# One expert's pair beside the small pair alone, in a mixture-of-experts stage on one core

## The chip, the cores and the metric

The kernel runs on one core of one Trainium2 chip. A core has a matrix engine (TensorE, PE in the profile), a vector engine (VectorE, DVE), an activation engine (ScalarE, ACT), GpSimd (POOL) and a queue engine (SyncE, SP) that issues the transfers here. Each runs its own instructions in order and waits for the others by semaphores. 16 DMA engines move data from HBM to the on-chip memory. The metric is the device time of one execution in microseconds (us); lower is better.

## The reference

Two layers of a backbone over 256 latent tokens with 256 context tokens, width 1024, all in float32. Each layer has a token mixer and a feed-forward part. The second layer's feed-forward part is a mixture of 8 experts, each token going to its best two:

```python
logits = (x @ router)
top_v, top_i = lax.top_k(logits, 2)
gates = einsum(softmax(top_v), one_hot(top_i, 8))
out = 0
for e in range(8):                      # wg, wu: 1024 x 3584, wd: 3584 x 1024
    out = out + gates[..., e:e + 1] * ((silu(x @ wg[e]) * (x @ wu[e])) @ wd[e])
```

It is followed by a residual and a layer norm. Only this mixture is touched by the change.

## The kernel before

**Pairs.** The tokens of each expert are gathered into blocks of up to 128, and the blocks stand in order of size, two to a pair, `a` to `d`. With the inputs measured, the first expert has more than 128 tokens and fills both blocks of pair `a` (kind 'one': up to 208 columns, one expert's weights for both blocks). Pair `b` ('whole') has two experts of up to 128 tokens, `c` ('mixed') one of up to 128 and one of up to 64, and `d` ('tiny') two of up to 32. Seven experts' weights are read, 588 transfers of 512 KB.

**Weights.** An expert's weights come in 84 units of 512 KB: 7 chunks of 512 hidden columns with 8 units each (4 of the gate matrix, 4 of the up matrix), numbered 0 to 55, and 28 units of the down matrix, 4 for each chunk. The generator `expert_halves` (L1400 on) loads them in the order of a plan into five raw buffers `rp` of 1 MB. For `b`, `c` and `d` a buffer holds the same unit of both experts (L1436); for `a` it holds the next two units of its one expert (L1428). For `a`, `b` and `c` each 512 KB is then split for precision: ScalarE rounds it to `hi` (L1413), VectorE subtracts to get `lo` (L1414). There are five buffers of each (`weight_pools(5, 5, 0)`). `d` is multiplied unsplit in float32, straight from the raw buffer, which therefore stays taken until TensorE has used it.

**Matmuls of one unit.** `b`: 12 of 512 columns (three products, hi x hi, hi x lo, lo x hi, for two blocks; L261 to L263). `c`: 10, since its small block needs two (L1514, L1515). `a`: 24 of 208 columns in the gate and up matrices (L1461), 12 of 512 in the down matrix. `d`: 8 of 256 columns on 32 columns of the array (L1590), 4 of 512 in the down matrix (L1625); the trace has two records for each. After a chunk's gate and up parts come the activation, the product, and a turning or a split (`c`: L1508, L1509, L1538, L1546, L1569, L588, L589; `a`: L1466, L1469, L255, L256; `d`: L1596, L1598, L1604).

**The order.** It is a string, `SCHEDULE[0]` for this distribution of tokens. `bu0123456` is the gate and up part of `b`, chunks 0 to 6, `bd...` its down part, `cp` starts the preparation (gathering and modulating its tokens) of `c`. Parts joined by `+` are worked on together: `merged` puts their units into one list, and by that list the weights are loaded and the matmuls written. Inside the block a scheduler then orders each engine's instructions by a model of their times, so that neighbouring units are interleaved further. When the last down part of a pair is written, its result is weighed and scattered to the tokens; for parts of a pair's down matrix the sums are kept (`partial`).

Of the kernel before, what the change touches and what calls it, by code (L numbers as in the profile page):

```python
# [28 lines left out]

ONE = 208  # L30
SCHEDULE = (
    'bu0123456 cp ap bd0123456 cu01+au0 cu23+au1 cu4 cu56+ad01 dp cd0123456+au2 du0123+au34 du456+ad234 '
    'dd0123+au56 dd45+ad56 dd6',
    'au0 bp au1 bu012 ad01 bu345 au2 bu6 cp bd0123456 au3 cu01 ad23 cu234 au4 cu56 dp cd0123456 au5 du0 '
    'ad45 du123 au6 du45 ad6 du6 dd0123456',
    'au0123456 bp ad0123456 bu0123456 cp bd0123456 cu0123456 dp cd0123456 du0123456 dd0123456',
# [89 lines left out]
def ahead(gen, n):  # L126

    q = deque()
    for item in gen:
        q.append(item)  # L130
        if len(q) > n:
            yield q.popleft()
    yield from q
# [25 lines left out]
class Net:  # L159
# [1531 lines left out]
    def partial(self, P, py):  # L1691

        nc = self.nc
        if P.kind == 'tiny':
            return
        first = P.sums is None
        if first:
            P.sums = [self.t4([128, 1024]) for _ in range(2)]
        for i in range(2):
            for hh in range(2):  # L1700
                s = P.sums[i][:, hh * 512:(hh + 1) * 512]
                if first:
                    nc.scalar.activation(s, py[i][hh], AF.Copy)
                else:
                    nc.vector.tensor_add(s, s, py[i][hh])
# [78 lines left out]
    def experts(self, routed, schedule, one=None, small=False):  # L1784

        nc, gms = self.nc, self.gms
        kinds = {0: 'whole' if one is None else 'one'}
        if small:
            kinds.update({STATIC_PAIRS - 2: 'mixed', STATIC_PAIRS - 1: 'tiny'})
        work = {'whole': self.gate_up, 'one': partial(self.gate_up_one, n=ONE if small else 256), 'mixed': self.gate_up_mixed, 'tiny': self.gate_up_tiny}

        def prep(j):
            kind = kinds.get(j, 'whole')
            return self.g_pair_prep(gms[:, j], None if j else self.long, 'whole' if kind == 'one' else kind)
        order = [[('abcd'.index(w[0]), w[1], [int(x) for x in w[2:]]) for w in t.split('+')]  # L1800
                 for t in schedule.split()]
        j0 = order[0][0][0]
        if j0:
            nc.vector.tensor_scalar_add(gms[:, j0], gms[:, 0], -256.0 * j0)
        preps = {j0: Side(prep(j0))}
        self.need(preps[j0])
        self.choices(*routed, j0)

        def m5():
            self.gate_row(1, 1, 'L', self.m5)  # L1810
            yield
        self.slow.append(Side(m5()))
        self.rate = 1.0
        span = {'u': (0, 8), 'g': (0, 4), 'h': (4, 8)}

        def units(j, w, cs):

            return [56 + 4 * c + k for c in cs for k in range(4)] if w == 'd' else \
                [8 * c + k for c in cs for k in range(*span[w])]

        def merged(parts):

            us = [units(*p) for p in parts]
            return [(i, u) for _, i, u in sorted(((k + 0.5) / len(v), i, u) for i, v in enumerate(us)
                                                 for k, u in enumerate(v))]

        def up(P, w, cs):
            for c in cs:
                if c not in P.work:
                    P.work[c] = work[P.kind](P, c)  # L1830
                    next(P.work[c])
                for _ in range(*span[w]):
                    yield
                    next(P.work[c], None)
            if w in 'uh' and cs[-1] == 6:
                P.act = P.shared = None

        steps = [t for t in order if t[0][1] != 'p']
        self.stream = ahead(self.expert_halves([(t[i][0], u) for t in steps for i, u in merged(t)], one,
                                               [j for j in kinds if kinds[j] == 'tiny']), 2)  # L1840
        pairs, sc, alpha = {}, None, ALPHA
        for n, parts in enumerate(order):
            if parts[0][1] == 'p':
                preps[parts[0][0]] = self.spawn(prep(parts[0][0]))
                continue
            last = n == len(order) - 1
            rows = [self.row(self.I[r][1]) for r in ('ln2_g', 'ln2_b')] if last else None
            gens = []
            self.tight = len(parts) > 1 and any(p[1] == 'd' for p in parts)
            for j, w, cs in parts:  # L1850
                if j not in pairs:
                    pairs[j] = self.start_pair(preps.pop(j), gms[:, j], kinds.get(j, 'whole'))
                tiny = pairs[j].kind == 'tiny'
                g = up(pairs[j], w, cs) if w != 'd' else \
                    self.down_tiny(pairs[j], cs) if tiny else self.down(pairs[j], cs, last)
                next(g)
                gens.append(g)
            for i, _ in merged(parts):
                j, w, cs = parts[i]
                try:  # L1860
                    next(gens[i])
                    continue
                except StopIteration as e:
                    py = e.value
                if w != 'd':
                    continue
                P = pairs[j]
                P.done += len(cs)
                if P.done < 7:
                    self.partial(P, py)  # L1870
                    continue
                ys, GT = self.weighed(P, py)
                sc = self.spawn(self.g_final(ys, GT, alpha, *rows) if last else self.g_scatter(ys, GT, alpha))
                alpha = 1.0
                del pairs[j], P
        self.need(sc)
        for w in list(self.side) + list(self.slow):
            self.need(w)
        self.side.clear()
        self.slow.clear()  # L1880
# [208 lines left out]
```

## Time and profile before

| | |
|---|---|
| three runs, median (lowest to highest) | 1970.03 us (1968.45 to 1970.07) |
| the profiled execution | 1970.38 us, span 1968.5 us |
| busy share of the span: PE, DVE, ACT, POOL | 96%, 69%, 54%, 3% |
| read from HBM | 515.64 MB, 262 GB/s over the span |

The profile's times count from the first instruction. The mixture begins at about 1084 us. A busy PE is counted with modelled ends, so neighbouring matmuls overlap in the rows: the cost of one is the time from its start to the start of the next. DMA share is the mean busy share of the 16 DMA engines.

### The profile page before, as it was taken

Reading aid. Unit: us, or ns where it says so; the run is one execution under the profiler, and the core shown is the slowest. Engines: PE = TensorE matmul, PEld = TensorE weight load, DVE = VectorE, ACT = ScalarE, POOL = GpSimd, SP = SyncE. Lnnn points to the kernel's source line nnn. Section 1 sums busy time; section 2 is a strip of 40 time slices with the busy share of each in tenths; the row PEclk is TensorE's granted clock in tenths of the full one; section 3 lists DMA queues with packets and bytes.
Section 4 is the critical chain, followed back from the end, with each engine's and each line's share of the span. In section 5 each row is a group of like instructions: output and inputs, shape, how many; then the busy total and the mean of one; then the engine's idle time right before and its main releaser. Section 6 shows DMA issues by size and latency. Waiting matters only on the chain. (4 is left out here: it accounts for less than half of the span.)

```text
span 1968.5 us, 28818 instructions
## 1 busy us (share of the span) xinstructions
PE 1886.0 (96%) x10399; PEld 1491.8 (76%) x10399; DVE 1348.6 (69%) x1970; ACT 1063.9 (54%) x1450; POOL 60.1 (3%) x68
## 2 busy tenths in 40 slices
PE   6999999999999999999997999999999999898995
PEld 3788877788888888878886788888887886655662
DVE  3887776688654564798777888999989885222325
ACT  3657645665322222466773877887787873211221
POOL 0100000000000000011000000000000000000000
PEclk9999999999999999999998899999999999999998
DMA  8653556576734442454440999989999999999984
GB/s 332 254 198 136 192 214 252 212 270 261 295 130 163 180 172 98 171 177 150 166 167 9 380 369 367 340 326 353 345 356 353 335 376 348 409 408 409 372 325 170
DMA packets 119022, 518.77 MB, mean 264 GB/s; under 512 B 14640, under 2 KB 15536, under 8 KB 95824
## 3 DMA queue, kind: packets, MB, share of 16 engines
q1 hardware_dynamic: 118864, 516.78, 70.3%
q8 instruction: 85, 1.39, 0.3%
q14 instruction: 73, 0.60, 0.1%
HBM read 515.64 MB, written 1.09 MB: 262 GB/s over the span
## 5 line engine op out<-in xcount | busy, mean ns | idle before, releaser
L262 PE MATMUL mm<-lo,t 128*128 128x512 f32 (+1 forms) x1560 | 608.7, 390 | 3.2 <-DVE lo L1414 1.7
L1414 DVE TENSOR_TENSOR lo<-rp,hi 128x1024 fp32r<-128x1024 f32 x420 | 492.7, 1219 | 167.9 <-ACT hi L1413 162.6
L263 PE MATMUL mm<-hi,t 128*128 128x512 f32 (+1 forms) x1560 | 603.3, 387 | 0.0
L261 PE MATMUL mm<-hi,t 128*128 128x512 f32 (+1 forms) x1560 | 584.1, 393 | 13.2 <-ACT hi L1413 6.6
L1413 ACT ACTIVATE hi<-rp 128x1024 fp32r<-128x1024 f32 (+1 forms) x420 | 424.9, 1056 | 80.7 <-PE mm L263 29.6
L255 ACT ACTIVATE hi<-raw 128x1024 fp32r<-128x1024 f32 x268 | 282.7, 1058 | 341.6 <-PE mm L263 184.5
L256 DVE TENSOR_TENSOR lo<-raw,hi 128x1024 fp32r<-128x1024 f32 x268 | 325.5, 1218 | 188.8 <-ACT hi L255 187.9
L261 PEld LDWEIGHTS mm<-hi,t 128*128 128x128 f32 x1560 | 292.0, 188 | 93.3 <-issue 17.6
L262 PEld LDWEIGHTS mm<-lo,t 128*128 128x128 f32 x1560 | 294.0, 189 | 73.7 <-DVE lo L1414 12.4
L263 PEld LDWEIGHTS mm<-hi,t 128*128 128x128 f32 x1560 | 293.9, 188 | 58.3 <-issue 1.2
L1017 PE MATMUL mm<-t,hi 128*128 128x512 f32 (+1 forms) x896 | 229.3, 345 | 0.0
L1017 PEld LDWEIGHTS mm<-t,hi 128*128 128x128 f32 x896 | 155.8, 189 | 29.1 <-issue 8.4
L1461 PE MATMUL mm<-t,hi 128*128 128x208 f32 x896 | 159.6, 280 | 5.8 <-ACT hi L1413 5.7
L1461 PEld LDWEIGHTS mm<-t,hi 128*128 128x128 f32 x896 | 136.2, 192 | 36.0 <-issue 20.6
L1017 PE MATMUL mm<-t,lo 128*128 128x512 f32 (+1 forms) x448 | 153.9, 344 | 0.0
L1461 PE MATMUL mm<-t,lo 128*128 128x208 f32 x448 | 118.2, 280 | 5.6 <-DVE lo L1414 5.6
L1461 PEld LDWEIGHTS mm<-t,lo 128*128 128x128 f32 x448 | 82.8, 193 | 14.3 <-DVE lo L1414 7.8
L1017 PEld LDWEIGHTS mm<-t,lo 128*128 128x128 f32 x448 | 84.8, 189 | 10.0
L313 POOL TENSOR_TENSOR sm<-sm,mhalf 128x1 f32<-128x1 f32 (+3 forms) x46 | 54.4, 1182 | 897.2 <-DVE sm L311 884.7
L266 PE MATMUL tr<-ident,t 128*128 128x128 f32 x376 | 59.4, 281 | 17.7 <-ACT t L344 16.1
L266 PEld LDWEIGHTS tr<-ident,t 128*128 128x128 f32 x376 | 45.7, 144 | 34.9 <-ACT t L344 19.7
L1590 PE MATMUL mm<-rp,t 128*32 128x256 f32 x896 | 70.4, 384 | 1.3 <-DMA rp<-in_expu 1.1
(287 smaller groups left out, 1686.4 us busy)
## 6 DMA issues: line engine op xcount, KB each, us to landing
rp<-in_expu SPq DMA_DIRECT2D x588, 512.0 KB
raw<-in_w_inu SPq DMA_DIRECT2D x64, 1024.0 KB
raw<-in_w_modu SPq DMA_DIRECT2D x44, 1024.0 KB
raw<-in_ffnu SPq DMA_DIRECT2D x42, 1024.0 KB
raw<-in_w_branchu SPq DMA_DIRECT2D x18, 1024.0 KB
raw<-in_w_outu SPq DMA_DIRECT2D x12, 1024.0 KB
t<-in_w_modu SPq DMA_DIRECT2D x8, 512.0 KB
t<-gd SPq DMA_DIRECT2D x7, 512.0 KB
```

Source lines behind the costliest of these rows:

```text
L255: self.nc.scalar.activation(hi, src, AF.Copy)
L256: self.nc.vector.tensor_sub(lo, src, hi.bitcast(F32))
L261: mm(out, ah, wh, start=first, stop=False)
L262: mm(out, ah, wl, start=False, stop=False)
L263: mm(out, al, wh, start=False, stop=last)
L266: self.nc.tensor.transpose(out, src, self.ident)
L313: self.nc.gpsimd.tensor_tensor(r, ve, self.mhalf[:, :n], op=OP.pow)
L1017: nc.tensor.matmul(out(t), a, x[p], start=kt + m + t % per == 0, stop=kt + m + t % per == (9 if per == 1 else 10))
L1413: nc.scalar.activation(hf, rs, AF.Copy)
L1414: nc.vector.tensor_sub(lf, rs if rv is None else rv, hf.bitcast(F32))
L1461: nc.tensor.matmul(out, a, x[p], start=kt + q + t % 2 == 0, stop=kt + q + t % 2 == 10)
L1590: nc.tensor.matmul(z[o:o + 32, :], x, raws[i][:, m, h * 256:(h + 1) * 256], start=k + m == 0, stop=k + m == 7)
```

## The change

```diff
 SCHEDULE = (
-    'bu0123456 cp ap bd0123456 cu01+au0 cu23+au1 cu4 cu56+ad01 dp cd0123456+au2 du0123+au34 du456+ad234 '
-    'dd0123+au56 dd45+ad56 dd6',
+    'bu0123456 cp bd0123456 cu0123456 dp ap cd0123456 du01+au01 du2+ad01 du34+au23 du5+ad23 du6+au4 dd0123+au56 '
+    'dd45+ad456 dd6',
...
-            return [(i, u) for _, i, u in sorted(((k + 0.5) / len(v), i, u) for i, v in enumerate(us)
+            return [(i, u) for _, i, u in sorted(((k // 2 * 2 + 1) / len(v), i, u) for i, v in enumerate(us)
                                                  for k, u in enumerate(v))]
```

Pair `a`, which stood beside `c` with three chunks up and two down and beside `d` with the rest, now stands beside `d` with all of it; `c` is worked on alone. `a` is prepared after `c`'s up part and not before `b`'s down part. The sort key of `merged` is the same now for two neighbouring units of a part, so two units of one pair are followed by two of the other. Nothing that is computed or loaded changes, only its order.

VectorE in `c`'s up part, one chunk: L1414 is a split, L1509, L1546 and L1569 belong to `c`'s activation, L1469 and L256 to `a`'s. Before:

```order
L1414 TENSOR_TENSOR lo<-rp,hi 128x1024
L1469 TENSOR_TENSOR u_12704<-u_12704,mm 128x2x208
L1469 TENSOR_TENSOR u_12706<-u_12706,mm 128x2x208
L1414 TENSOR_TENSOR lo<-rp,hi 128x1024
L1569 TENSOR_TENSOR u_12897<-u_12897,mm 128x512
L256 TENSOR_TENSOR t_13031<-u_12704,t_13030 128x2x208
L256 TENSOR_TENSOR t_13031<-u_12706,t_13030 128x2x208
L1414 TENSOR_TENSOR lo<-rp,hi 128x1024
L1509 TENSOR_TENSOR u_13083<-t_13084,mm 64x512
```

The same place now:

```order
L1414 TENSOR_TENSOR lo<-rp,hi 128x1024
L1569 TENSOR_TENSOR u_12810<-u_12810,mm 128x512
L1414 TENSOR_TENSOR lo<-rp,hi 128x1024
L1414 ISA
L1414 TENSOR_TENSOR lo<-rp,hi 128x1024
L1509 TENSOR_TENSOR u_12927<-t_12928,mm 64x512
L1414 TENSOR_TENSOR lo<-rp,hi 128x1024
L1546 TENSOR_TENSOR u_12827<-u_12827,u_12927 64x512
```

`a`'s instructions are gone from among `c`'s, and what is left is `c`'s own splits and activation (ISA sets a register).

ScalarE in `d`'s gate and up part: L1413 is a split of `a`'s weights, L1466 and L255 `a`'s activation and split, L1596 and L1604 `d`'s activation and the copy of its turned result; L1596, L1466 and L1604 wait for TensorE. Before:

```order
L1596 ACTIVATE u_15844<-mm 128x256
L1413 ACTIVATE hi<-rp 128x1024 x2
L255 ACTIVATE t_15941<-u_15718 128x2x208
L255 ACTIVATE t_15941<-u_15720 128x2x208
L1604 ACTIVATE t_15447<-tr 128x256
L1413 ACTIVATE hi<-rp 128x1024 x2
L1596 ACTIVATE u_16071<-mm 128x256
L1413 ACTIVATE hi<-rp 128x1024 x2
```

Now:

```order
L1413 ACTIVATE hi<-rp 128x1024 x3
L1596 ACTIVATE u_15066<-mm 128x256
L1413 ACTIVATE hi<-rp 128x1024
L1466 ACTIVATE u_15124<-mm 128x2x208
L1466 ACTIVATE u_15126<-mm 128x2x208
L1413 ACTIVATE hi<-rp 128x1024 x4
L1604 ACTIVATE t_14503<-tr 128x256
L255 ACTIVATE t_15299<-u_15124 128x2x208
L255 ACTIVATE t_15299<-u_15126 128x2x208
```

Where two splits stood between any two of `d`'s instructions, three or four now stand ahead of the one that waits.

TensorE at the start of a group in the same part, L1461 being `a` and L1590 `d` (in the trace each L1590 has two records). Before:

```order
L1461 MATMUL mm<-t_11704,hi 128x208
L1590 MATMUL mm<-rp,t_14519 32x256 x8
L1461 MATMUL mm<-t_11703,lo 128x208
L1461 MATMUL mm<-t_11703,hi 128x208
L1461 MATMUL mm<-t_11704,hi 128x208
L1461 MATMUL mm<-t_11703,lo 128x208
L1461 MATMUL mm<-t_11703,hi 128x208
L1461 MATMUL mm<-t_11704,hi 128x208
L1590 MATMUL mm<-rp,t_14519 32x256 x6
```

Now:

```order
L1461 MATMUL mm<-t_13930,hi 128x208
L1461 MATMUL mm<-t_13929,lo 128x208
L1590 MATMUL mm<-rp,t_13759 32x256 x14
L1461 MATMUL mm<-t_13867,hi 128x208
L1461 MATMUL mm<-t_13868,hi 128x208
L1461 MATMUL mm<-t_13867,hi 128x208
L1461 MATMUL mm<-t_13868,hi 128x208
L1461 MATMUL mm<-t_13867,lo 128x208
```

Two units of `d` (16 matmuls) now stand as 14 in a row and 2 ahead of them, between 48 matmuls of `a`: 28, then the 2, then 20, then the 14.

## Rows read from the trace of the kernel before

**Rows 1.** Busy time by stage: PE, PEld, DVE, ACT, POOL, PEclk, DMA, GB/s.

```profile
1091.00:1343.00 252.00, 251.02 (x1170) 206.64 (x1169) 225.06 (x234) 207.86 (x255) 0.48 (x2) 1.00 0.96 362
1343.00:1638.00 295.00, 293.56 (x1614) 248.47 (x1613) 265.33 (x265) 233.00 (x272) 1.55 (x6) 1.00 0.94 353
1638.00:1740.00 102.00, 92.94 (x888) 63.80 (x886) 31.77 (x40) 24.45 (x34) 1.29 (x5) 1.00 0.98 380
1740.00:1821.00 81.00, 71.78 (x580) 41.34 (x580) 20.59 (x23) 15.99 (x20) 0.26 (x1) 1.00 1.03 409
1821.00:1936.00 115.00, 111.33 (x685) 69.93 (x680) 36.61 (x39) 30.67 (x37) 0.00 (x0) 0.99 0.94 350
```

**Rows 2.** Lines of `c` and `d` alone: count, duration ns, first and last start.

```profile
L1514 PE MATMUL mm<-hi,t x168: 387/389/500, 1346.9 to 1638.5; 128*128 128x512 f32 x168
...
L1590 PE MATMUL mm<-rp,t x896: 376/379/404, 1638.8 to 1820.7; 128*32 128x256 f32 x180
...
L1625 PE MATMUL mm<-rp,t x224: 590/592/859, 1820.7 to 1944.5; 128*32 128x512 f32 x112
```

**Rows 3.** Chain that ended last: start us, us, what it waited for.

```profile
1788.26 9.84 DMA rp<-in_expu
```

**Rows 4.** Busy time in the `cu4` stretch, all engines; then VectorE's splits alone.

```profile
1467.00:1490.00 23.00, 22.52 (x99) 16.46 (x98) 22.81 (x24) 19.17 (x24) 0.00 (x0) 1.00 1.01 377
...
1467.00:1490.00 23.00, 18.74 (x16) 1.00 1.01 377
```

**Rows 5.** Chain that ended last, matmuls of 512 columns in `b`, of 208 in `a`.

```profile
1316.31 0.45 PE mm L261 x2
...
1328.55 0.45 PE mm L261 x2
...
1612.62 2.21 PE mm L1461 x20
```

**Rows 6.** Timeline of VectorE around `cu4`: start us, us, instruction.

```profile
1464.52 0.68 DVE L1569 TENSOR_TENSOR u<-u,mm 128x512 f32<-128x512 f32 x1
...
1466.25 1.08 DVE L256 TENSOR_TENSOR t<-u,t 128x416 fp32r<-128x416 f32 x2
1467.25 1.22 DVE L1414 TENSOR_TENSOR lo<-rp,hi 128x1024 fp32r<-128x1024 f32 x1
...
1478.92 6.90 DVE L1414 TENSOR_TENSOR lo<-rp,hi 128x1024 fp32r<-128x1024 f32 x6
1485.74 0.68 DVE L1569 TENSOR_TENSOR u<-u,mm 128x512 f32<-128x512 f32 x1
```

**Rows 7.** Timeline of TensorE, `d`'s gate and up matmuls among `a`'s.

```profile
1661.58 0.62 PE L1590 MATMUL mm<-rp,t 128*32 128x256 f32 x4
1662.13 0.47 PE L1461 MATMUL mm<-t,hi 128*128 128x208 f32 x2
...
1666.67 1.92 PE L1590 MATMUL mm<-rp,t 128*32 128x256 f32 x28
```

**Rows 8.** Timeline of TensorE, `d`'s down matmuls among `a`'s.

```profile
1904.54 1.05 PE L1625 MATMUL mm<-rp,t 128*32 128x512 f32 x4
1905.52 0.50 PE L262 MATMUL mm<-lo,t 128*128 128x512 f32 x1
...
1907.57 1.91 PE L1625 MATMUL mm<-rp,t 128*32 128x512 f32 x12
1909.41 1.21 PE L261 MATMUL mm<-hi,t 128*128 128x512 f32 x4
...
1913.30 1.05 PE L1625 MATMUL mm<-rp,t 128*32 128x512 f32 x4
```

**Rows 9.** Chain, a preparation's matmuls; group of the residual's multiplications: count, busy us, mean ns.

```profile
1280.46 1.87 PE tr L1296 x16
...
L885 DVE TENSOR_TENSOR t<-mm,m 128x512 f32<-128x512 f32 x16 | 10.2, 684 | 3.6 <-PE mm L1361 2.7 <-PE mm L1357 0.7
```

**Rows 10.** Timeline of TensorE, `a` after a half chunk; in brackets the wait.

```profile
1672.23 0.36 PE L1461 MATMUL mm<-t,lo 128*128 128x208 f32 x1 [0.56 <-DVE lo L1414]
```

## The prediction

> **What bounds the kernel now.** Start with the busy time by stage [rows 1]. From 1091 us to the end four stages follow each other, and their edges come from the first and last starts of the lines that only one pair uses [rows 2]: `b` alone to 1343, `c` with part of `a` to 1638, the first half of `d` (its gate and up units) with part of `a` to 1821, the second half of `d` (its down units) with the rest of `a` to 1936. TensorE is busy for 251.0 of 252 and 293.6 of 295 us in the first two, for 92.9 of 102 and 71.8 of 81 in the third, and for 111.3 of 115 in the fourth. So only the third has time to win on TensorE, some 18 us by the busy column. In its last 81 us the DMA engines show a share of 1.03 at 409 GB/s, and the chain of waits steps from transfer to transfer, 9.8 us each with four or so in the queue [rows 3]. A unit of `d` is 1.049 MB, so 2.57 us at that rate, and there are 56: the third stage moves 56 of them and 28 half-size units of `a`, 73.4 MB, 180 us of its 183. It is bound by transfers.
>
> The next thing to look at is the one stretch in which `c` stands alone already, `cu4`, 1467 to 1490 [rows 4]. VectorE is busy 22.81 of 23.00 us there and makes 16 splits, which is exactly one chunk of `c`'s up part (8 units, two halves each). TensorE is still at 22.5, because it works off what had been prepared before. So `c` without `a` beside it is bound by VectorE, and with `a` it is not (265 of 295 us in the second stage). These two facts are the whole question: the change takes `a` out of the stage that it relieves of VectorE and puts it into the stage that it relieves of DMA.
>
> **Prices.** A matmul of 512 columns: 54 of them between two rows of the chain, 12.24 us, 0.2267 us each [rows 5]. One of `a`'s 208 columns: 2.21 us for 20, 0.1105 [rows 5]. VectorE in one chunk of `c`'s up part: from one multiplication L1569 to the next it is never idle, 21.22 us, with 15 splits and two subtractions of `a` that go (1.00 us, 1466.25 to 1467.25); six splits in a row take 6.82 us, 1.137 each, so with 16 splits and without `a` a chunk is 21.4 us [rows 6]. `d`'s matmuls: a run of four records costs 0.55 us to the next instruction, 28 records 1.92 us [rows 7]; I take 1.84 for the latter, since the modelled end overshoots (4 records show 0.62 and cost 0.55). In its down part the runs cost 0.98 and 1.84, and the 8 and 16 matmuls of 512 between them 2.05 and 3.89, that is 0.23 and 0.26 above their price, the cost of going from the small shape to the large one [rows 8].
>
> **Part by part.** First, `a`'s preparation leaves the `b` stage: 32 matmuls, 16 in 1.87 us [rows 9], 3.7 us off. That stage is bound by TensorE, so it ends that much earlier; the work comes back in `cd`, where TensorE has slack.
>
> Second, `c` alone. VectorE: 7 chunks up, 149.5 us; 7 chunks down with 8 splits and one 512-column subtraction, 7 x (9.1 + 0.6) = 67.9; about twenty more instructions of some 0.68 us [rows 9] for the end of `b`, the two preparations and the gates, 14. That is 231 us. TensorE needs 840 matmuls, 190 us, and 16 or so for turning, scattering and preparing: 206. The five buffers for split weights are full when `b` ends, which takes 5 x 1.137 off, and after the last split TensorE has 1.4 us left. So 227, and at the 99% of `cu4` I take 228. In the order that the changed program has, VectorE's reads of TensorE's results stand one or two splits behind the split that they need, so little is added. Bounds: 222 (no loss at all and preparation hidden) and 248 (each up chunk takes the 23.0 us of `cu4` whole, 161, and the down chunks go at that stretch's 377 GB/s, 78; with the 14 and less 5).
>
> Third, `a` wholly beside `d`. The order shows the groups: 28 of `a` matmuls, 2 of `d`, 20 of `a`, 14 of `d`. In the trace each `d` matmul is two records, so a group is 48 x 0.1105 + 0.55 + 1.84 + two changes of shape at 0.2 = 8.1 us for two units of each. With `a`'s down units it is 3.89 + 0.55 + 2.05 + 1.84 = 8.3. With both pairs' last parts it is 48 x 0.1105 + 0.98 + 1.84 + 0.4 = 8.5 (up) and 8.76 (down, as measured from 1904.54 to 1913.30). There are 20, 8 and 8 of the first three, and the 144 matmuls of `a`'s last down units come with ten units of `d` in five groups, one of them with 48 and not 24 matmuls (14.2): 162.0 + 66.6 + 68.2 + (4 x 8.76 + 14.2) = 346. Beside them: `d`'s turning 4, `c`'s scatter 5, gates and the change of stage 3, and a wait at each end of a half chunk of `a`, where the next split stands behind the reads of the finished one in ScalarE's order. Such a wait is 0.56 us [rows 10]; 14 at 0.5 make 7. Sum 365, less 0.9 since the last run of `d` is shorter: 364. Bounds: 355 (no wait) and 385 (waits of 1.5 us at each half chunk and 7 us of waiting for data).
>
> Transfers in that stage: 88 MB in the 28 first groups, 240 us with the small terms, 367 GB/s, under the 409 seen. The five raw buffers matter more. `a`'s two units come in one buffer, and it is freed by the first `d` unit of the group before, at that group's end. So `a`'s next data have one group, 8.1 us, less 2.4 for the two split instructions, and need 2.6 plus the two transfers before them. By this count there are about 2 us to spare.
>
> Together: before, from 1343 to 1936, 593 us. After: 228 + 364 = 592, and 3.7 less ahead of it, gives 4 to 5 us less. The profiled execution took 1970.4 (span 1968.5 and 1.9 around it), which lies 0.35 us above the median of the runs. Forecast: 1966 us. Most of what the third stage gives back is lost again in `c`: 18 us or more of TensorE's waiting for transfers go, and 22 us of its waiting for VectorE (228 less 206) come; the rest comes from fewer half-chunk waits and from the two halves of the stage now sharing one pace.
>
> [...]
>
> **Rivals.** *`c` goes at the pace of the stream* (slower). VectorE, ScalarE and the transfers are all within 10% of each other in `c` alone: 8.39 MB a chunk is 20.5 us at 409 GB/s and 22.3 at 377, against 21.4 on VectorE. If they do not overlap fully the stage takes the upper bound of 248, and the time is 1966 + 20 = 1986; it decides from 23.0 us a chunk. For it: the share of 1.01 at 377 GB/s. Against it: VectorE did not wait in `cu4`, and five raw buffers are full when the stage begins.
>
> *The raw buffers hold back `d` with `a`* (slower). If `a`'s transfer is queued behind both of `d`'s, it lands after the group has ended, and each of the 28 first groups waits, say 0.6 us: 17 us, 1983. For it: 9.8 us from issue to landing when the queue is full [rows 3], more than a group. Against it: the queue is full only where transfers are the bound, and in the fourth stage the same one-to-one mix ran at 350 GB/s without a transfer in the chain.
>
> *Both stages at their lower bounds* (faster): 222 + 355, 15 us less than forecast, 1951. For it: ScalarE's order after the change has three of four splits ahead of `d`'s activation, where before two of each four stood behind it, and the row of [rows 10] is such a wait. Against it: turning and partial sums of `a` cost something in every stage seen.
>
> **How the numbers follow.** Forecast case 0.50 (its own range 1959 to 1973), stream 0.18, buffers 0.15, lower bounds 0.17. This kernel's measurement can tell 0.2%, 3.9 us, from no change, so the forecast sits on that edge. Faster: half of the forecast case and the lower bounds, 0.25 + 0.17 = 0.42. Same: 0.20 of the forecast case, and 0.09 of the two slow ones where they cost little, 0.29. Slower: the rest, 0.29. The range runs from 1950 to 1984: it leaves out the stream case where it costs its full price, and what lies under the lower bounds.
>
> **What would show it.** Right: in `c` alone VectorE busy over 95% and TensorE about 90%, a chunk of its up part at 21 to 22 us, the stage's length at 225 to 233; then TensorE over 95% to the end, DMA share about 0.95, the mixed stage at 358 to 368. Wrong: a chunk at 23 us with VectorE waiting for ScalarE and that for transfers, or transfers in the chain of waits while `d` and `a` run, or TensorE without waits in `c`.

## Result, and the profile after

The changed kernel takes 1982.38 us (median of four runs, 1982.15 to 1983.38), the kernel before 1970.05 (1968.45 to 1970.08) beside it. The ratio is 1.0061, 95% interval 1.0049 to 1.0073: 12 us slower, where 1966 was forecast. The profiled execution has a span of 1981.6 us, 13.1 more than before.

Busy time by stage, with the columns of [rows 1]: `b`, `c` alone, `d`'s gate and up part with `a`, `d`'s down part with `a`.

```profile
1091.00:1341.00 250.00, 247.87 (x1133) 202.88 (x1133) 221.31 (x237) 202.36 (x242) 0.00 (x0) 0.99 0.97 369
1341.00:1581.00 240.00, 227.54 (x995) 169.32 (x993) 229.25 (x235) 199.33 (x239) 1.30 (x5) 0.99 0.95 356
1581.00:1826.00 245.00, 235.57 (x2038) 174.62 (x2035) 87.36 (x96) 75.64 (x96) 2.28 (x9) 1.00 0.97 363
1826.00:1949.00 123.00, 122.31 (x778) 82.26 (x779) 43.63 (x45) 34.90 (x40) 0.00 (x0) 1.00 0.93 344
```

First and last starts of the lines that only one pair uses, as in [rows 2].

```profile
L1514 PE MATMUL mm<-hi,t x168: 387/391/507, 1345.3 to 1580.4; 128*128 128x512 f32 x168
```

```profile
L1590 PE MATMUL mm<-rp,t x896: 379/379/403, 1580.7 to 1823.7; 128*32 128x256 f32 x180
```

```profile
L1625 PE MATMUL mm<-rp,t x224: 592/592/617, 1828.6 to 1957.7; 128*32 128x512 f32 x112
```

`b` ends at 1341.7, 1.3 us earlier than before (3.7 were expected). `c` alone takes to the first L1590 at 1580.7: 239 us, not 228. The last L1625 starts at 1957.7 and not 1944.5; it stood 8.5 us behind the stage's edge of 1936 before, so `d`'s stage ends at 1949.2: 368.5 us, not 364. The transfers bind nothing in it any more: its chain of waits has no transfer. So `b`, `c` and `d` missed by 2.4, 11 and 4.5 us, 18 in all; `d`'s stage ends 13 us later, where the terms of the forecast had it end 4 to 5 us earlier.

The 239 us of `c` in two parts, up part and down part, with the columns of [rows 1]:

```profile
1341.70:1502.00 160.30, 150.53 (x629) 108.08 (x628) 154.87 (x160) 131.87 (x157) 0.00 (x0) 1.00 0.97 361
1502.00:1580.70 78.70, 76.02 (x361) 60.53 (x359) 73.39 (x76) 66.76 (x82) 1.30 (x5) 0.98 0.93 346
```

VectorE is busy for 228.3 us. The forecast had 225 (231 less the five splits that are ready at the start) and allowed some 3 for idle time. So 3 us of the miss are work that was not counted, and VectorE is idle for 10.7 us, one half in the up part and one half in the down part.

The steady state of `c`'s up part, which before could be seen for one chunk only [rows 4, 6], is this. Timeline of VectorE and then of ScalarE (start us, us, instruction, in brackets the idle time before and what ended it).

```profile
1430.85 0.69 DVE L1569 TENSOR_TENSOR u<-u,mm 128x512 f32<-128x512 f32 x1 [0.40 <-PE mm L263]
...
1444.34 1.23 DVE L1414 TENSOR_TENSOR lo<-rp,hi 128x1024 fp32r<-128x1024 f32 x1 [0.82 <-ACT hi L1413]
1445.60 0.68 DVE L1509 TENSOR_TENSOR u<-t,mm 64x512 f32<-64x512 f32 x1
1446.31 6.90 DVE L1414 TENSOR_TENSOR lo<-rp,hi 128x1024 fp32r<-128x1024 f32 x6
1453.64 0.69 DVE L1569 TENSOR_TENSOR u<-u,mm 128x512 f32<-128x512 f32 x1 [0.43 <-PE mm L263]
```

```profile
1442.76 0.60 ACT L1566 ACTIVATE u<-mm 128x512 f32<-128x512 f32 x1 [1.85 <-PE mm L263]
1443.26 1.05 ACT L1413 ACTIVATE hi<-rp 128x1024 fp32r x1
```

The gate's silu L1566 stands too early in ScalarE's order. ScalarE waits 1.85 us for the gate's last matmul; the next hi can't begin before 1443.26, the lo behind it not before 1444.34, and VectorE stands idle for 0.82 us. At the up part's end L1569 makes VectorE itself wait, 0.43 us. From L1569 at 1430.85 to L1569 at 1453.64 a chunk takes 22.8 us, 1.4 more than the 21.4 of VectorE's work that were forecast; the two waits make 1.25 of that. It is so in the last four chunks of the up part; the first ones still live on splits that stood ready. VectorE and TensorE wait for each other in a ring: TensorE for a lo (6.0 us in 15 waits from 1365 to 1502), the read of its sums for TensorE (1.85 us here), the next hi for that read, the next lo for that hi (0.82).

The same in `d`'s stage, the chain of waits (start us, us, what) at a half chunk of `a` (L1466) and at a chunk end of `d` (L1598). A chunk end of `a` (L1469, at 1726.75) has much the same steps.

```profile
1708.62 0.02 ACT u L1466
...
1709.03 1.06 ACT hi L1413
...
1710.12 1.24 DVE lo L1414
...
1711.39 2.93 PE mm L1461 x24
1714.33 0.56 PE mm L1590 x4
1714.88 2.42 PE mm L1461 x20
1717.30 1.88 PE mm L1590 x28
...
1719.20 0.03 DVE u L1598
...
1719.53 1.23 DVE lo L1414
...
1720.81 2.93 PE mm L1461 x24
```

The prices of [rows 7] hold (0.56 and 1.88 for `d`'s runs; 2.42 for 20 of `a`'s, the change of shape among them). But where a read stands ahead of a split, the 28 matmuls of `a` that should follow at once begin late: behind `d`'s run that ends at 1719.18, 24 of the 28 begin only at 1720.81.

### The profile page after: what moved, and what is told of

Same layout as the page of the kernel before. It is cut to its first block, busy times and chain, and to the rows that moved or that the text cites. A ratio compares the mean times of both kernels' runs of the same rounds, so it can differ in the third digit from the quotient of the medians.

```text
span 1981.6 us, 28818 instructions
## 1 busy us (share of the span) xinstructions
PE 1899.2 (96%) x10399; PEld 1490.3 (75%) x10399; DVE 1350.9 (68%) x1970; ACT 1064.3 (54%) x1450; POOL 60.2 (3%) x68
## 5 line engine op out<-in xcount | busy, mean ns | idle before, releaser
L1414 DVE TENSOR_TENSOR lo<-rp,hi 128x1024 fp32r<-128x1024 f32 x420 | 494.1, 1220 | 166.0 <-ACT hi L1413 158.6
L1413 ACT ACTIVATE hi<-rp 128x1024 fp32r<-128x1024 f32 (+1 forms) x420 | 424.6, 1056 | 131.3 <-DMA rp<-in_expu 99.2
L255 ACT ACTIVATE hi<-raw 128x1024 fp32r<-128x1024 f32 x268 | 282.7, 1058 | 343.6 <-PE mm L263 190.1
L256 DVE TENSOR_TENSOR lo<-raw,hi 128x1024 fp32r<-128x1024 f32 x268 | 325.6, 1219 | 186.7 <-ACT hi L255 185.7
L1017 PEld LDWEIGHTS mm<-t,hi 128*128 128x128 f32 x896 | 155.8, 189 | 29.1 <-issue 8.4
L1461 PE MATMUL mm<-t,hi 128*128 128x208 f32 x896 | 152.9, 277 | 0.7 <-ACT hi L1413 0.7
L1461 PEld LDWEIGHTS mm<-t,hi 128*128 128x128 f32 x896 | 131.3, 192 | 15.5 <-issue 7.0
L1461 PE MATMUL mm<-t,lo 128*128 128x208 f32 x448 | 118.0, 284 | 7.5 <-DVE lo L1414 7.4
L1461 PEld LDWEIGHTS mm<-t,lo 128*128 128x128 f32 x448 | 81.2, 191 | 25.4 <-issue 14.1
L266 PEld LDWEIGHTS tr<-ident,t 128*128 128x128 f32 x376 | 46.4, 145 | 35.4 <-ACT t L344 19.5
L1590 PE MATMUL mm<-rp,t 128*32 128x256 f32 x896 | 71.7, 384 | 0.0
```

The source lines that it names most:

```text
L255: self.nc.scalar.activation(hi, src, AF.Copy)
L256: self.nc.vector.tensor_sub(lo, src, hi.bitcast(F32))
L266: self.nc.tensor.transpose(out, src, self.ident)
L1017: nc.tensor.matmul(out(t), a, x[p], start=kt + m + t % per == 0, stop=kt + m + t % per == (9 if per == 1 else 10))
L1413: nc.scalar.activation(hf, rs, AF.Copy)
L1414: nc.vector.tensor_sub(lf, rs if rv is None else rv, hf.bitcast(F32))
```

## The experiments

Theory 1 is that ring: reads of TensorE's sums that stand too early in the in-order queues of ScalarE and VectorE. Theory 2 is the rival *stream* of the prediction, which fits the same chunk of 22.8 us: 8.39 MB at 365 to 387 GB/s with a DMA share of 0.98 to 1.00.

**1. Half of c's transfers.**

```diff
-            for i in range(2):
+            cut = isinstance(j, int) and j == STATIC_PAIRS - 2 and one is not None
+            for i in range(1 if cut else 2):
                 nc.sync.dma_start(raw[:, i, :], self.I['expu'][ds(ex[i], 1), u].squeeze(0),
...
-            yield 1, *parts(u, *(raw[:, ds(ldb[k], 1), :].squeeze(1) for k in ('scalar', 'vector')))
+            yield 1, *(parts(u, raw[:, 0, :]) if cut else
+                       parts(u, *(raw[:, ds(ldb[k], 1), :].squeeze(1) for k in ('scalar', 'vector'))))
```

> The changed kernel, but c loads only its first expert's units and splits each of them twice, so the second expert's weights are left out of the result; splits, matmuls and activations are as many as before, and c's transfers are halved (44 instead of 88 MB). In the changed kernel a chunk of c's up part takes 22.8 to 23.0 us and the whole stage of c 239 us, where 21.4 and 228 were forecast. Theory 1 (loop): VectorE's 21.4 us of work a chunk plus some 1.4 us in which VectorE waits for a split of ScalarE, which stands behind a read of TensorE's sums, for which TensorE waits in turn for a split of VectorE. A chunk then stays at 22.6 to 22.9 us. Only the down part, where ScalarE waits for transfers 13 times, gets some 3 us shorter; the stage is 234 to 237 us, the program 3 to 5 us faster than the changed kernel. Theory 2 (stream): c goes at the pace of transfers that reach only 372 GB/s while splits run. A chunk then falls to 21.4 to 21.6 us, the stage to 224 to 228, the program by 11 to 15 us.

Measured: 1969.95 us in one run (before: 1972.2), most chunks 21.36 us, VectorE busy 22.84 of 23 us. That looks like theory 2. But the scheduler, which models the transfers too, had put the reads in another order: the copy L588 that follows the up part stands behind the next gate's silu here, not ahead of it, and that silu itself stands two splits later. Two things were changed at once, and run 8 takes them apart.

**2. No wait for the sums.**

```diff
+            s = [self.xs[0][0][:, 512 * h:512 * h + 512].bitcast(F32) for h in range(2)]
...
-                nc.scalar.activation(g, z[0], AF.Silu)
-                P.flat[c] = self.spawn_first(gate(z[1]))
+                nc.scalar.activation(g, s[0], AF.Silu)
+                P.flat[c] = self.spawn_first(gate(s[1]))
```

(and so for the two reads of the up part)

> The changed kernel, but in c's gate and up part the four reads of TensorE's sums (ScalarE's silu of the first block and copy of the second, VectorE's two multiplications and additions) read a tile that is there from the start, so that they wait for no matmul; c's hidden values are wrong by that. Matmuls, splits, activations and transfers are as many as in the changed kernel. Theory 1 (loop): the waits of some 1.4 us a chunk go, VectorE is busy over 98%, a chunk of c's up part falls from 22.8 to 21.4 to 21.7 us, the seven of them by 8 to 10 us. Theory 2 (stream): transfers are as before, a chunk stays at 22.5 to 22.9 us and ScalarE waits for transfers instead.

Measured: 1983.59 us, `c`'s stage again 239 us. It decides nothing: with nothing to wait for, the scheduler moved the multiplications of six chunks into the first 70 us, where they held up the splits, and the transfers that were late then bound the end.

```profile
1342.00:1433.00 91.00, 78.34 (x339) 57.14 (x338) 89.28 (x106) 76.23 (x100) 0.00 (x0) 0.94 0.79 291
...
1502.00:1580.00 78.00, 76.01 (x307) 55.36 (x306) 75.86 (x68) 65.46 (x66) 1.03 (x4) 1.00 1.03 408
```

TensorE is busy for 78 of the first 91 us, and the DMA engines run at 1.03 and 408 GB/s at the end. A read that no longer waits is another program.

**3. Half of VectorE's splits in c.**

```diff
             nc.scalar.activation(hf, rs, AF.Copy)
+            if cut:
+                return hi, hi
```

(`cut` for the second expert of `c`, as in run 1)

> The changed kernel, but for c's second expert VectorE makes no lo; its matmuls use hi in its place, so that part of the result has less precision. VectorE's splits in a chunk of c's up part fall from 16 to 8, its work from 21.4 to about 12.3 us; ScalarE's work (18.6), TensorE's (80 matmuls at 0.2267 and the turning, about 19) and the transfers (8.39 MB) stay. Theory 1 (loop): without the bound on VectorE a chunk falls to what is next, transfers at 409 GB/s or TensorE, 19.5 to 21 us; c's stage to 215 to 225. Theory 2 (stream): a chunk stays at 22.3 to 22.9 us, at 365 to 377 GB/s.

Measured: 1971.56 us, most chunks 21.36 us, the first matmul of `d` at 1568.7, 12 us earlier. All of `c`'s bytes came, at 377 to 397 GB/s, so theory 2's pace (372) is no limit of the transfers. But neither 19.5 us nor theory 1's stage was fully reached: ScalarE waits for TensorE at two reads there (its silu and its copy of the sums, L1569 and L1511 of this run's kernel, 1.2 to 1.3 us each), so VectorE's work is not all that can set the chunk. VectorE is busy for only 12.8 of 21.5 us, and yet the chunk is as long as in run 1, where VectorE is never idle: the length of a chunk alone doesn't tell what sets it.

**4 to 7. The two edits apart, and another order.** Run 4 is the kernel before with the new sort key alone, run 5 the changed kernel with the old key, runs 6 and 7 a third order with either key. The third order against the changed one:

```diff
-    'bu0123456 cp bd0123456 cu0123456 dp ap cd0123456 du01+au01 du2+ad01 du34+au23 du5+ad23 du6+au4 dd0123+au56 '
-    'dd45+ad456 dd6',
+    'bu0123456 cp ap bd0123456 cu0123+au0 cu456+au1 dp cd0123456 du0+ad01 du12+au2 du34+au3 du5+ad23 du6+au4 '
+    'dd0123+au56 dd45+ad456 dd6',
```

> The kernel before with the new sort key alone: two units of each by turns, the old order of parts. If both edits take part in the loss, this is 2 to 5 us slower than before; if the loss is all in the moving of a away from c (what the trace shows: 11 us in c alone, 4 in the stage of d), it is within 2 us of before, since VectorE and transfers have the same work in every stage.

> The changed order of parts with the old sort key: a unit of each by turns. c alone is the same in both, so its 239 us stay. If the loss is in the moving of a, this is 9 to 15 us slower than before, like the changed kernel; if the key costs d's stage its 4 us (waits at each half chunk), it is 8 us slower than before.

> A third order, with the new key: two chunks of a's gate and up part stand beside c (au0 beside cu0123, au1 beside cu456), all the rest of a beside d. By the theory that VectorE in c and transfers with d are two idle times that a's work can fill: VectorE's work in c's up part goes up by 16 splits, but TensorE's by 2 x 8 x 24 x 0.11 = 42 us, so c's up part is bound by TensorE (127 + 42 + small terms, about 180 us with VectorE at 150 + 20), and d's stage is shorter by 42 us and still has fewer transfers than TensorE time. c with a: about 255, d with a: 320 to 325; together 575 to 580, against 593 before and 607 after. Expected 1952 to 1962 us, 8 to 18 faster than before. If the two idle times can't be filled (stream theory: transfers at 372 GB/s bound both), 1968 to 1975.

> The same third order with the old key, a unit of each by turns. If the key makes no difference, within 2 us of the run with the new key; if the new key's longer runs of one shape save changes of shape, 3 to 6 us slower than that.

| order of parts | old key | new key |
|---|---|---|
| before | 1970.0 | 1966.74, ratio 0.9983 (0.9974 to 0.9992) |
| changed | 1993.14, ratio 1.0118 (1.0102 to 1.0133) | 1982.38, ratio 1.0061 (1.0049 to 1.0073) |
| third | 1977.47, ratio 1.0035 (1.0023 to 1.0048) | 1972.30, ratio 1.0012 (1.0002 to 1.0021) |

Each ratio is to the kernel before as it was measured beside that run. The key is a gain in every row, 3 to 4, 11 and 5 us; the moving of `a` is the loss. Runs 4 and 5 both missed what was expected: the key alone was not to gain, and the order alone was to lose 8 to 15 us and lost 22. What the key does in `d`'s stage is seen in the chain of waits of run 5: a group has three runs of `d` and takes 8.45 us (1694.94 to 1703.39), where the changed kernel's has two and takes 8.13 (1627.53 to 1635.66, a group without waits).

```profile
1694.94 0.56 PE mm L1590 x4
...
1696.90 0.99 PE mm L1590 x12
...
1699.30 1.00 PE mm L1590 x16
...
1703.39 0.56 PE mm L1590 x4
```

The third order missed the expected 1952 to 1962: `c` with `a` ended 6 us later than counted (1604 for 1343 and 255), `d` with `a` took 332 and not 320 to 325, with TensorE waiting 13 us there for splits (run 6). Columns: who waits for whom, us in total, times, longest.

```profile
PE mm L1461 <- ACT hi L1413: 7.3, 6, 1.4
PE mm L1461 <- DVE lo L1414: 5.8, 12, 0.7
```

**8. Half of c's transfers, same order of instructions.** The flag that makes the second expert be loaded is set to zero on the chip, which the scheduler doesn't see.

```diff
         V.tensor_mul(self.ldb, ld, valid[:, :, 1])
+        V.memset(self.ldb[:, STATIC_PAIRS - 2:STATIC_PAIRS - 1], 0)
```

> The changed kernel with one instruction more, far ahead of the experts, that sets the flag by which c's second expert is loaded to zero: its transfers are skipped and its splits read the first expert's units, so its weights are left out of the result. The order of the instructions on every engine is that of the changed kernel; in the first run with half of c's transfers the scheduler had also put the reads of TensorE's sums in other places. A chunk of c's up part takes 22.8 us in the changed kernel. Theory 1 (loop of in-order waits): the chunk stays at 22.6 to 22.9 us with 1.3 us of VectorE's waits in it; only the down part gets shorter, by 3 to 6 us. Theory 2 (stream): the chunk falls to 21.4 to 21.6 us, VectorE never waits, c's stage falls by 11 to 14 us.

Measured: 1980.09 us in one run. A chunk stays at 22.76 us (L1570 at 1429.81 and 1452.57). One chunk of the changed kernel, and then of this one, with the columns of [rows 1], and this one's waits of VectorE from 1365 to 1502:

```profile
1433.00:1456.00 23.00, 21.68 (x90) 15.18 (x90) 21.62 (x22) 18.79 (x24) 0.00 (x0) 1.00 0.98 365
```

```profile
1433.00:1456.00 23.00, 21.69 (x91) 15.21 (x91) 21.65 (x22) 18.81 (x23) 0.00 (x0) 1.00 0.57 183
```

```profile
DVE lo L1415 <- ACT hi L1414: 2.5, 3, 0.8
DVE u L1570 <- PE mm L263: 2.0, 5, 0.4
```

At 183 GB/s and a share of 0.57 every engine is as busy as at 365, and VectorE's waits are the same (2.5 and 2.1 in the changed kernel). Theory 2 falls for the up part. Only the down part got shorter, as theory 1 has it; `d` begins at 1577.4, 3.3 us earlier. Of these, 1.0 was there when `c`'s up part ended (its last L1570 at 1498.44, L1569 at 1499.45 in the changed kernel), so the down part is shorter by 2.3, a little less than the 3 to 6 expected. So some 2 of the 11 us that `c` missed hang on transfers in the down part; one of 7.0 us stands in the changed kernel's chain of waits there.

**9. Late reads in c.** In the program `issue_after` puts an instruction behind another in its engine's order without a wait for it.

```diff
-            nc.scalar.activation(hf, rs, AF.Copy)
-            nc.vector.tensor_sub(lf, rs if rv is None else rv, hf.bitcast(F32))
+            self.hi_ins = nc.scalar.activation(hf, rs, AF.Copy)
+            self.lo_ins = nc.vector.tensor_sub(lf, rs if rv is None else rv, hf.bitcast(F32))
...
-        def gate(z):
-            yield from item(z)
+        def gate(g, z, z1):
+            for _ in range(LATE):
+                yield
+            with self.tc.issue_after(self.hi_ins.ins):
+                nc.scalar.activation(g, z, AF.Silu)
+            yield from item(z1)
```

(LATE is 2; the copies and multiplications likewise)

> The changed kernel with c's reads of TensorE's sums put one or two splits later in ScalarE's and VectorE's order: the silu of the first block after 2 more units have been split, the copies and multiplications likewise. Nothing else changes. Theory 1 (loop): ScalarE's and VectorE's waits for TensorE get shorter, a chunk of c's up part falls from 22.8 to 21.5 to 22.2 us, the program by 4 to 9 us. Theory 2 (stream): the chunk stays at 22.5 to 22.8 us, the program within 2 us of the changed kernel.

Measured: 1974.53 us, ratio to before 1.0022 (1.0013 to 1.0032), 7.9 less than the changed kernel (5.5 between the two profiled spans). Timeline of VectorE and of ScalarE, and one chunk's busy times:

```profile
1431.56 0.68 DVE L1550 TENSOR_TENSOR u<-u,mm 128x512 f32<-128x512 f32 x1
...
1443.11 0.68 DVE L1510 TENSOR_TENSOR u<-t,mm 64x512 f32<-64x512 f32 x1
1443.83 9.18 DVE L1415 TENSOR_TENSOR lo<-rp,hi 128x1024 fp32r<-128x1024 f32 x8
1452.92 0.68 DVE L1550 TENSOR_TENSOR u<-u,mm 128x512 f32<-128x512 f32 x1
```

```profile
1435.95 3.89 ACT L1414 ACTIVATE hi<-rp 128x1024 fp32r x4
1439.75 0.60 ACT L1542 ACTIVATE u<-mm 128x512 f32<-128x512 f32 x1
```

```profile
1433.00:1456.00 23.00, 22.36 (x97) 16.11 (x96) 22.87 (x23) 19.57 (x25) 0.00 (x0) 1.00 1.01 403
```

The silu (L1542 here) stands two splits later and waits for nothing; VectorE is never idle from 1365 to 1502; a chunk is 21.36 us, the forecast's 21.4. The transfers follow at 403 GB/s. In the up part ScalarE's and VectorE's order differs from the changed kernel's only in where the reads of TensorE's results stand among the splits; the scheduler also let some of TensorE's matmuls, and behind the up part some instructions of `a`'s preparation, change places. `c`'s stage begins 0.6 us earlier and ends 5.6 us earlier (first L1598 at 1575.1): 234 us, 5 of the 11 back. `d`'s stage is as long as before this edit, 368.6 us. The 6 us that are left come from the down part, where VectorE is still idle for 6.1 us, most of it waiting for ScalarE's hi (5.4), and from 2 us of work on VectorE that was not counted. ScalarE works on `a`'s preparation in the down part too; how much of its lateness is due to that and how much to transfers, no run separates.

**10. Four raw buffers, six for each half of a split.**

```diff
-            with self.tc.block(schedule_with_timeline_sim=True), self.weight_pools(5, 5, 0):
+            with self.tc.block(schedule_with_timeline_sim=True), self.weight_pools(4, 6, 0):
```

> The changed kernel with four raw buffers and six buffers each for hi and lo, in place of five and five; the order of the instructions in c's stage is unchanged. Theory 1 (loop): ScalarE and VectorE can be one split further ahead of TensorE when a read of sums comes, worth about 1.1 us a chunk: 21.4 to 22.0 us. Theory 2 (stream): one buffer less holds the transfers back more, the chunk takes 22.8 us or longer, up to 24.

Measured: 1987.7 us in one run, the chunk 22.76 us, as in the changed kernel. What theory 1 expected, 21.4 to 22.0, missed; theory 2's 22.8 or longer is met at its lower end, so this run doesn't speak against theory 2, which rests on run 8. The sixth buffer doesn't help; the order fits that, since the silu stands ahead of the next hi however many buffers are free. Four raw buffers make `c`'s chunk no longer. `d`'s stage is 4.5 us longer (373.0), and its chain of waits has eight transfers of 5.8 to 8.1 us, where the changed kernel's has none.

**11 and 12. Late reads for all three pairs**, in the changed order and in the third: the edit of run 9 for `a`'s activations (6 units later in the program) and `d`'s (4 units later).

> The changed kernel with the reads of TensorE's sums put one or two splits later for all three pairs, not for c alone: the activations and multiplications at a's half chunks and at d's chunk ends too. In the changed kernel d's stage took 368.4 us, 4.4 more than forecast, and TensorE's chain of waits goes through ScalarE's and VectorE's reads at each half chunk (1.0 to 1.3 us each, where 0.5 was counted). Theory 1 (in-order waits in d's stage as well): that stage falls by 4 to 10 us, the program to 1965 to 1971. Theory 2 (in d's stage the loss is in changes of shape and transfers, not in these waits): that stage stays within 2 us of 368, the program within 2 us of the run with late reads for c alone, 1974.5.

> The third order (two chunks of a's gate and up part beside c, the rest beside d, new key), 1972.3 us, with the late reads for all three pairs. Its trace showed 4 us of waits for splits while c and a run and 16 us while d and a run. Theory 1 (in-order waits): 1958 to 1967 us, faster than the kernel before. Theory 2: within 3 us of 1972.

Measured: 1959.03 us, ratio to before 0.9942 (0.9929 to 0.9956), faster than both kernels; and 1963.83, ratio 0.9965 (0.9951 to 0.9979). In the changed order the late reads for `a` and `d` bring `d`'s stage from 368.5 down to 353.0 us, 15.5 less where 4 to 10 were expected. TensorE's waits in it, of the changed kernel and of run 11:

```profile
PE mm L1461 <- DVE lo L1414: 7.4, 15, 0.7
PE tr L266 <- DVE u L1598: 1.1, 2, 0.5
PE mm L261 <- ACT hi L1413: 0.7, 2, 0.4
PE mm L1461 <- ACT hi L1413: 0.7, 2, 0.4
```

```profile
PE mm L1474 <- DVE lo L1417: 0.7, 2, 0.5
```

And the chain of waits of run 11, which is TensorE alone (L1474 is `a`, L1618 `d`):

```profile
1698.11 3.31 PE mm L1474 x28
1701.42 0.56 PE mm L1618 x4
1701.98 2.42 PE mm L1474 x20
1704.39 1.85 PE mm L1618 x28
1706.24 3.31 PE mm L1474 x28
```

A group is 8.13 us, the forecast's 8.1, and now there is nothing between groups. The 9.9 us of waits in the first of these two tables are less than the 15.5 us that went. TensorE's busy time in the stage fell too, from 357.9 to 351.9 us for the same matmuls: part of the delay had been counted as busy time, and a sum of waits leaves that out. In the third order (run 12) `c` got 9 us faster and `d`'s stage stayed at 333 us. There TensorE still waits for hi, lo and transfers, and with part of `a` away its waits for transfers, of which run 11 has none, come to 6.3 us:

```profile
PE mm L1618 <- DMA rp<-in_expu: 6.3, 11, 1.7
PE mm L1474 <- ACT hi L1416: 5.6, 4, 1.5
PE mm L1474 <- DVE lo L1417: 3.2, 8, 0.6
```

**13 and 14. The order before with the same late reads**, with the old and the new key.

> The kernel before (old order of parts, old key) with the late reads of e11 for c, a and d. By the theory that the waits cost time only where TensorE is neither kept busy by a second pair's prepared splits (c with a: 1.2 us of TensorE's waits in 296) nor waits for transfers (d with a to 1821), only the last 115 us, d's down part with a, can gain: some 4 to 10 us of waits of TensorE for splits there and none before. 1962 to 1969 us. If the late reads are a gain of their own in every stage, 1955 to 1960.

> The kernel before with the new key and the late reads of e11 (the old order of parts). The key alone came to 1966.7 us. By the theory 1960 to 1966: the third stage stays bound by transfers, the last one loses its waits. If it comes to 1959 or less, moving a to d is worth nothing even without waits.

Measured: 1966.59 us, ratio 0.9984 (0.9975 to 0.9993), and 1968.90, ratio 0.9993 (0.9984 to 1.0002). The late reads are worth 3.7 us in the order before and 23 in the changed one (1982.38 to 1959.03). In run 13 `c`'s stage beside `a` gains nothing (297 us, 296 before); `d`'s stage gains 6 us, 3.8 of them in its down part. With late reads in both, the whole change is a gain of 7.6 us (1966.59 to 1959.03), and the moving of `a` alone, with the new key on both sides, one of 9.9 (1968.90 to 1959.03). In run 14 TensorE still waits, in the third stage for transfers, as expected, but the run missed the 1960 to 1966. Its third stage takes 190 us, with the key alone 184 (run 4) and with late reads alone 180 (run 13); TensorE's waits for transfers in it are 8.3, 5.5 and 2.1 us. Why key and late reads don't add up there stayed open.

```profile
PE mm L1618 <- DMA rp<-in_expu: 8.3, 15, 1.2
PE mm L264 <- ACT hi L1416: 7.9, 5, 2.4
```

## Why the prediction was wrong

**The step that failed** is the sentence on `c` alone: "In the order that the changed program has, VectorE's reads of TensorE's results stand one or two splits behind the split that they need, so little is added." It looked at VectorE's reads alone. ScalarE's silu stands ahead of the hi that VectorE needs next, and in this stage, which VectorE bounds, what delayed VectorE was added. It came to 1.4 us a chunk in the last four chunks, and run 9, which moves the reads, takes it away: 5 of the 11 us that `c` missed. The other 6 lie in the down part and in VectorE's work. The sum had hardly any wait of VectorE there, and put `a`'s preparation there because TensorE has slack; but VectorE waited 4.2 us for ScalarE's hi, part of which hangs on transfers (run 8 takes 2.3 us off), and its work was 3 us more. The bounds of 222 and 248 held, but the value was taken near the lower one. The evidence for it, VectorE busy for 22.81 of 23 us [rows 4], was one chunk at the start of which TensorE still had `a`'s prepared work to do; by this account the ring closes only when that work is gone and TensorE waits for VectorE all the time. Before, with `c` beside `a`, TensorE waited for splits only 1.2 us of 296, and moving the same reads gained nothing there (run 13).

**The half-chunk waits in d's stage** were mis-sized by the same error: 7 us were counted, from one row of 0.56 us [rows 10] for the 14 half chunks of `a`. Run 11 took 15.5 us away. `d`'s chunk ends, where L1598 stands ahead of a lo, were not counted at all. What the sum says without waits, 357, measured 353.0. So the 4.5 us by which this stage missed are a larger error, 8.5, with 4 us too many elsewhere against it; that it looked nearly right was luck. *Both stages at their lower bounds* came true by half for a program with late reads: `d`'s stage took 353 in run 11 (355 was the bound), `c`'s 232 (222); its price was 1951, and run 11 took 1959.

**The b stage** ended 1.3 us earlier and not 3.7. The preparation did go; but the trace shows the first matmul of `b`'s up part 1.3 us later (1094.11, before 1092.80), and TensorE waiting 2.1 us for lo up to the end of `b`, before 1.0. That makes up the 2.4 us; why it came so, no run tested.

**Right**: VectorE's work in a chunk (21.4), the prices of matmuls and groups (8.1), and the loss in `c` eating what the third stage gives. That third stage was bound by transfers: in the changed order it is not any more (no transfer in the chain of waits). The new key was thought of as part of the move; alone it is a gain of 3 to 4 us (run 4), and in the changed order it is worth 11 us (run 5). A group is 0.32 us shorter, which would make 9 of them if all of the 28 first groups are like the two compared.

**The rivals.** *Stream* had nearly the right time, 1986, by a wrong cause: run 8 halves the transfers and the chunk stays (22.76 us). The trace had looked like it, with a DMA share of 0.98 to 1.00. Run 9 moved 403 GB/s through a chunk while the splits ran, above the 377 that was counted for this rival. *The raw buffers* cost nothing with five, since no transfer stands in the chain in `d`'s stage; with four, transfers stand in it (run 10).

That a split ready to run waits behind a read that is not, is what the trace shows at 1442.76 to 1443.26 and what run 9 undoes: ScalarE waits 1.85 us ahead of the silu, and the hi behind it, which has no wait of its own, begins only at 1443.26; with the silu two splits later VectorE is never idle from 1365 to 1502.

## What to carry to other kernels

When a change takes away the second pair that kept TensorE busy, look at every read of TensorE's sums in the in-order queues of the engines that feed TensorE: here such a read cost nothing while TensorE had other prepared work (run 13, `c` beside `a`: 297 us with the reads moved, 296 before), and its wait was added to the chunk when it had not (22.8 us in the changed kernel, 21.36 in run 9). Read it from a steady state, not from one chunk at the seam of two stages, and count such reads on all engines. A DMA share of 0.98 to 1.00 did not say that transfers were the bound here; skipping half of them without touching the order of instructions told it (0.57, and a chunk still of 22.76 us, run 8), and leaving out a load in the program let the scheduler write another one (run 1).

## What the runs showed of the hardware that was not expected

The DMA engines showed a share of 0.98 to 1.00 at 365 to 387 GB/s in chunks of the changed kernel's up part where transfers bound nothing (run 8), and 1.01 at 403 in the chunk of run 9: a share of 1.0 did not tell how much more the transfers could move. VectorE's busy time in a chunk was the same at 183 and at 365 GB/s, 21.65 and 21.62 us, so at these rates the traffic into the on-chip memory did not slow its splits.
